# Encoder trunk on one core: where VectorE's low parts, convolution taps, gate blocks and edge zeros stand in the queues

## The chip, the cores and the metric

One core of a Trainium2 chip runs the whole trunk: two layers over 768 tokens, in float32 products that are put together from rounded high and low parts. The metric is device microseconds of one execution, as the median of several runs. Differences under about 0.2% (5 us) can't be told from no change.

## The reference, cut to what matters

```python
def trunk(x, ...):                       # x: (1, 256, 1024) and (1, 512, 1024), same weights
    for l in range(DEPTH):               # DEPTH = 2
        h = rms_norm(x, g_mix[l])
        q, k, v, u, gl = jnp.split(h @ w_in[l], splits, axis=-1)
        q = apply_axial_rope(rms_norm(q, g_q[l]), cos, sin)
        k = apply_axial_rope(rms_norm(k, g_k[l]), cos, sin)
        a = blocked_attention(q, k, v)   # 8 heads of 128, 2 kv heads, softmax over all keys
        c = conv_module(u, ...)          # a * sigmoid(g); depthwise conv of 31 taps;
                                         # layer norm over channels; silu; @ w_pw
        ga, gc = jnp.split(jax.nn.sigmoid(gl + b_gate[l]), 2, axis=-1)
        x = x + (ga * a + gc * c) @ w_out[l]
        gate, up = jnp.split(rms_norm(x, g_ffn[l]) @ w_gu[l], 2, axis=-1)
        x = x + (silu(gate) * up) @ w_down[l]
    return rms_norm(x, g_final)
```

## The kernel before

A product of two float32 matrices is made of three passes: high x high, low x high, high x low. ScalarE rounds a loaded weight tile of 128x1024 into its high part (line 211), and the low part, tile minus high, is written by VectorE (line 133) or GpSimd (line 214). `Unit.make` does this for one tile. `Weights` holds at most `N_WS` = 4 loaded tiles that are not yet split, and `split` counts a tile as used once its high and low parts have been issued.

Each layer has a mixing half and a feed-forward half. In the mixing half the program issues blocks in the order of the list `FILL`: `ag:j` makes the two halves of the input of convolution channel block j (128 channels), `gl:i` a gate block, and `k`, `v`, `q:i` the attention's inputs. The first seven blocks run alone. The other 22 are poured between the steps of the attention: one step for each head h and each token tile t (48 steps, named h0t0 to h7t5 in the tiles), with `FILL_US` microseconds of block work for each step. When `FILL` is used up, the output products of the convolution, `pw:0` to `pw:7`, are poured in its place.

An attention step issues its scores, then VectorE's row maximum, ScalarE's exponential, GpSimd's reciprocal of the sum (line 1332, tile `st`) and ScalarE's scaling. TensorE transposes the result (tile `T`, line 207) one step later.

The convolution of a channel block is 30 taps on VectorE, each one instruction over 783 columns (tile `L_y<-L_z`), after ScalarE did the first. Tile `L_z` holds the gated input with 15 zero columns at the start, between the two sequences and at the end. There are `N_Z` = 3 such tiles. When `ag_half` wants a fourth, it issues taps at once until the oldest convolution's last tap has been issued (the loop with `clock.tap()`), and then GpSimd writes the three strips of zeros of the new tile (line 803). Otherwise the taps come from `Clock.tick`: it counts TensorE's columns at 2400 to the microsecond as its time, adds up a cost for each VectorE instruction (elements / 960 plus 0.13 us; for a tap 783 / 960 + `TAP_MORE`), and issues taps as long as VectorE's sum is less than `TAP_AHEAD` = 1 us ahead.

After the eighth convolution `channel_norm` follows: mean (TensorE, tile `L_mean`), centring, squares, variance (TensorE, tile `L_var`), the spread of the reciprocal root, scaling, silu, and the split into `L_zsh` and `L_zsl`, which `pw:0` needs (tile `L_c`). When `pw:0` is reached and the norm is not done, `Clock.force` issues all that is left of it on the spot, ahead of any further TensorE work.

All engines run their own queue in the order in which the program issued. The quoted lines are those that the steps below touch most:

```python
while y.z_live >= N_Z:          # ag_half
    clock.tap()
...
for o in (0, PAD + NP, ZP - PAD):
    nc.gpsimd.memset(part["z"][:, o:o + PAD], 0.0)
...
self.clock.vector(n / 960.0 + (TAP_MORE if n == CONV_N else 0.13))     # Vector
```

Of the kernel before, what the change touches and what calls it, by code (L numbers as in the profile page):

```python
# [30 lines left out]
PAD = CK // 2  # L31
# [87 lines left out]
class Vector:  # L119
# [5 lines left out]
    def __getattr__(self, name):  # L125
        f = getattr(self.engine, name)

        def call(out, *args, **kw):
            n = 1
            for d in (args[0].shape if name == "tensor_reduce" else out.shape)[1:]:  # L130
                n *= d
            self.clock.vector(n / 960.0 + (TAP_MORE if n == CONV_N else 0.13))
            return f(out, *args, **kw)  # L133
# [22 lines left out]
def trunk(tc, x_in, x_tok, w_a, w_qkv, w_pw, w_out, w_gu, w_down, vecs, gqk, rope, y_out):  # L156
    nc = tc.nc
    clock = Clock()
    vector = Vector(nc.vector, clock)

    with ExitStack() as ctx:
# [15 lines left out]
        def U(name, dtype=F32):  # L177
            return UC(name, dtype)[:, :T]

        def Z(name, n=ZP, dtype=F32):  # L180
            return wpool.tile([P, n], dtype, name=name, tag="z", bufs=N_Z)
# [28 lines left out]
        def act(out, in_, func=AF.Copy, **kw):  # L210
            nc.scalar.activation(out, in_, func, **kw)  # L211

        def sub_lo(engine, lo, x, hi):
            engine.tensor_tensor(lo, x, hi.bitcast(F32), op=ALU.subtract)  # L214
# [6 lines left out]
        class Stage:  # L221


            def __init__(self, name, src):
                self.name, self.src, self.tile, self.last = name, src, None, None
# [5 lines left out]
        class Unit:  # L231
# [2 lines left out]

            def __init__(self, name, stages):
                self.name, self.stages, self.out, self.live = name, stages, None, False
                for stage in stages:
                    stage.last = self

            def make(self, engines):  # L240
                hi = wpool.tile([P, 1024], F32R, name="hi_" + self.name, tag="w", bufs=N_W)
                lo = wpool.tile([P, 1024], F32R, name="lo_" + self.name, tag="w", bufs=N_W)
                stage = self.stages[0].tile
                act(hi, stage)
                n = 1024 // len(engines)
                for i, e in enumerate(engines):
                    sl = slice(i * n, (i + 1) * n)
                    sub_lo(e, lo[:, sl], stage[:, sl], hi[:, sl])
                self.out = (hi, lo)

        class Quarter(Unit):

# [6 lines left out]
            def make(self, engines):  # L259
                src = self.quad.operand(self.m)  # L260
                both = wpool.tile([P, 1024], F32R, name="wq_" + self.name, tag="w", bufs=N_W)
                hi, lo = both[:, :512], both[:, 512:]
                act(hi, src)
                sub_lo(engines[0], lo, src, hi)
                self.out = (hi, lo)

        class Quad:

# [19 lines left out]
        class Weights:  # L288
# [36 lines left out]
            def split(self, engines=(nc.gpsimd,)):  # L325
                w = self.all[self.ready]
                while not self.here(w):
                    assert self.load()
                assert self.live + w.size + max(self.staged, N_WS) <= N_W
                self.live += w.size  # L330
                w.live = True
                w.make(engines)
                self.staged -= sum(stage.last is w for stage in w.stages)
                self.ready += 1
                self.next = max(self.next, clock.now + W_STEP[w.size - 1])

            def pump(self):
                while self.load():
                    pass
                if self.ready < len(self.all) and clock.now >= self.next:  # L340
                    w = self.all[self.ready]
                    if self.here(w) and self.live + w.size + max(self.staged, N_WS) <= N_W:
                        self.split(self.engines(w))
# [5 lines left out]
            def get(self, w):  # L349
                while w.out is None:  # L350
                    self.split(self.engines(self.all[self.ready]))
                return w.out

            def free(self, w):
# [60 lines left out]
        weights = Weights()  # L415
# [86 lines left out]
        def proj_two(ws, hT, s, names, parts=SPLITS):  # L502

            t0, n = parts[s]
            ps = [PS(name) for name in names]
            for k in range(KC):
                for w, o in zip(ws, ps):
                    for p, (a, b) in enumerate(PASSES):
                        mm(o[:, :n], w[a][:, k * P:(k + 1) * P], hT.cols(k, b, s),
                           k == 0 and p == 0, k == KC - 1 and p == 2)  # L510
                if k % 2 and k < KC - 1:
                    yield
            yield
            return ps
# [118 lines left out]
        def layer_blocks(l):  # L633
# [127 lines left out]
            def conv(j, z):  # L761
                wcol = lambda k: vcol(l, V_WDW, k * KC + j)

                def first():
                    y.y[j] = UC(nm(f"y{j}"))
                    act(y.y[j], z[:, :CONV_N], AF.Identity, scale=wcol(0), bias=vcol(l, V_BDW, j))
# [23 lines left out]
                def ready():  # L790
                    first()
                    clock.at(FIRST_AT[1], lambda: clock.waiting.append(taps))
                clock.at(FIRST_AT[0], ready)

            def ag_half(j, ws, w0, s, part):
                if s == 0:
                    while y.z_live >= N_Z:
                        clock.tap()
                    y.z_live += 1
                    part["sg"] = U(nm(f"sg{j}"))  # L800
                    part["z"] = Z(nm(f"z{j}"))
                    for o in (0, PAD + NP, ZP - PAD):
                        nc.gpsimd.memset(part["z"][:, o:o + PAD], 0.0)
                sg, z = part["sg"], part["z"]
                t0, n = SPLITS[s]
                y.norm.need(s)
                if l in TWO_AG and (j, s) == (0, 0):
                    pg, pa = yield from proj_two([ws[w0], ws[w0 + 1]], y.hT, s, [nm(f"ug{j}_{s}"), nm(f"ua{j}_{s}")])
                    act(sg[:, t0:t0 + n], pg[:, :n])
                else:  # L810
                    pg = yield from proj_a(ws[w0], y.hT, s, nm(f"ug{j}_{s}"))
                    act(sg[:, t0:t0 + n], pg[:, :n])
                    pa = yield from proj_a(ws[w0 + 1], y.hT, s, nm(f"ua{j}_{s}"))
                act(z[:, ZOFF[s]:ZOFF[s] + n], pa[:, :n])
                if s == 0:
                    return
                ws.free(w0, w0 + 1)

                def gate():
                    for s, (t0, n) in enumerate(SPLITS):  # L820
                        zz = z[:, ZOFF[s]:ZOFF[s] + n]
                        vector.tensor_tensor(zz, zz, sg[:, t0:t0 + n], op=ALU.mult)
                    conv(j, z)

                def sig(dt):
                    act(sg, sg, AF.Sigmoid)
                    clock.at(dt, gate)
                y.sig.append((True, sig))
# [11 lines left out]
            def gl_body(idx):  # L840
                def body(ws):
# [3 lines left out]
                    for s, (t0, n) in enumerate(SPLITS):  # L845
                        pg = yield from proj_a(ws[0], y.hT, s, nm(f"gl{idx}_{s}"))
                        act(sg[:, t0:t0 + n], pg[:, :n])
                        if s == 0 and FILL[-1] == f"gl:{idx}":
                            y.h_free = 1
# [9 lines left out]

            for b in FILL:  # L860
                kind, _, n = b.partition(":")
                n = int(n or 0)
# [434 lines left out]
        def attention(y):  # L1297
# [7 lines left out]
            def scores(n):  # L1305
# [22 lines left out]

                late = stream.done((l, FILL[-1]))
                jobs[n] = [  # L1330
# [55 lines left out]
            def fill():  # L1386
                goal[0] += FILL_US / 2
                if not stream.done((l, FILL[-1])):
                    stream.run(goal[0], (l, FILL[-1]))
                    if stream.done((l, FILL[-1])):  # L1390
                        goal[0] = stream.work
                        goal[0] += PW_START
                        y.late = clock.now + 8.0
                        y.h_free = 2
                        split_z(y)
                elif y.m_done:
                    goal[0] = max(goal[0] + (LATE_US - FILL_US) / 2, stream.work)
                    stream.run(goal[0], (l, f"pw:{min(y.m_done, PW_MAX) - 1}"))
# [21 lines left out]
        def channel_norm(y):  # L1420
# [59 lines left out]
            def scale(j):  # L1480
                def f():
                    for s, (t0, n) in enumerate(SPLITS):
                        sl = slice(YO[s], YO[s] + n)
                        vector.tensor_tensor(ys[j][:, sl], ys[j][:, sl], rstd[s][:, :n], op=ALU.mult)
                    if j in SILU_AT:
                        clock.at(0.5, lambda: silus(j))
# [126 lines left out]
        clock.drain()  # L1613


FILL = ["ag2", "k", "q:0", "gl:0", "ag:4", "ag:2", "ag:3", "gl:8", "v", "gl:9", "gl:1", "q:1", "ag:5", "ag:6",
        "gl:10", "gl:2", "q:2", "ag:7", "gl:3", "gl:14", "gl:12", "gl:4", "gl:11", "q:3", "gl:5", "gl:13", "gl:7",
        "gl:15", "gl:6"]
SILU_AT = (5, 7)
FIRST_AT = (1.2, 1.4)  # L1620
BURSTS = ((1, 7), (6, 4), (5, 2), (3,))
D_FIRST = (4.0, 6.0)
# [11 lines left out]
BEFORE = 7  # L1634
SIG_MAX = 3
SIG_LEFT = 25
FILL_US = 6.3
LATE_US = 3.7
PW_MAX = 10
PW_START = 3.0  # L1640
# [6 lines left out]
RSTD_AFTER = 5.4  # L1647
TABLES_AT = 16.0
TAP_AHEAD = 1.0
TAP_MORE = 0.13  # L1650
W_STEP = (0.9, 2.9)
A_EXP = 2.2
A_REC = (3.5, 2.5)
# [91 lines left out]
```

## Time and profile before

| | us |
|---|---|
| median of 3 runs | 2441.3 (2438.95 to 2444.44) |
| the profiled execution, its own time | 2443.3 |
| its span in the trace | 2441.5 |
| TensorE busy | 2226.4 (91%) |
| VectorE busy | 1876.5 (77%) |
| ScalarE busy | 1143.8 (47%) |
| GpSimd busy | 1068.2 (44%) |
| mean granted TensorE clock | 0.959 of full speed |

The span has four parts: layer 0's mixing half (to about 700 us), its feed-forward half (to about 1210), and the same two of layer 1. The waits of one layer's mixing half return in the other's almost to the tenth of a microsecond, so one layer is read and counted twice.

### The profile page before, as it was taken

To read this page: it belongs to the slowest core of one execution; us is meant where nothing else is said; L and a number is where in the kernel's file an instruction comes from. 1 tells how busy PE (TensorE), PEld (TensorE's weight loads), DVE (VectorE), ACT (ScalarE), POOL (GpSimd) and SP (SyncE) were. 2 spreads that over 40 slices of the span, in tenths; PEclk is the share of its full clock that TensorE was granted. 3 is DMA by queue.
4 is the path that set the end of the run, shared out by engine and by line. 5 is a ranking of instruction groups with operands and counts; after the bars stand their busy time and mean duration, and the time that the engine had idled before them with its cause. 6 is when DMAs were issued, how large, how long until landed. Compare 5 with 4: busy or idle time off the path is not lost. (4 is left out here: it accounts for less than half of the span.)

```text
span 2441.5 us, 34896 instructions
## 1 busy us (share of the span) xinstructions
PE 2226.4 (91%) x13276; PEld 2095.6 (86%) x13276; DVE 1876.5 (77%) x2484; ACT 1143.8 (47%) x2289; POOL 1068.2 (44%) x935
## 2 busy tenths in 40 slices
PE   8999869949979999999989998698699799999997
PEld 7989859848979999999988898596589799999997
DVE  5899768956387788798968897689553877987888
ACT  5446536555244444444443555465642444444443
POOL 3704132311256666666445142131112666666663
PEclk9999989969989999999999999899799899999998
DMA  4112111213312343343421111112142133333332
GB/s 165 61 57 69 66 39 63 77 43 113 133 49 90 121 144 116 124 145 113 152 85 61 63 63 57 50 63 72 54 146 101 35 121 127 124 130 137 122 123 87
DMA packets 72423, 229.59 MB, mean 94 GB/s; under 512 B 8128, under 2 KB 15296, under 8 KB 72256
## 3 DMA queue, kind: packets, MB, share of 16 engines
q1 hardware_dynamic: 72256, 227.37, 27.1%
q8 instruction: 104, 1.70, 0.3%
q14 instruction: 63, 0.52, 0.1%
HBM read 208.46 MB, written 18.87 MB: 93 GB/s over the span
## 5 line engine op out<-in xcount | busy, mean ns | idle before, releaser
L133 DVE SCALAR_TENSOR_TENSOR L_y<-L_z,vec,L_y 128x783 f32<-128x783 f32 x480 | 496.1, 1077 | 0.8
L214 POOL TENSOR_TENSOR wq_L_wgu_0m<-T_L_wgu,wq_L_wgu_0m 128x512 fp32r<-128x512 f32 x168 | 228.6, 1376 | 173.8 <-ACT wq_L_wgu_0m L211 173.8
L211 ACT ACTIVATE wq_L_wgu_0m<-T_L_wgu 128x512 fp32r<-128x512 f32 x168 | 102.7, 630 | 259.3 <-DVE T_L_wgu L133 208.7
L214 POOL TENSOR_TENSOR wq_L_wgu_0m<-st_L_wgu,wq_L_wgu_0m 128x512 fp32r<-128x512 f32 x126 | 179.3, 1425 | 43.4 <-ACT wq_L_wgu_0m L211 42.7
L203 PE MATMUL L_gl<-L_h1h,hi_L_wgl 128*128 128x512 f32 (+1 forms) x512 | 176.6, 345 | 0.0
L203 PE MATMUL L_gl<-L_h1h,lo_L_wgl 128*128 128x512 f32 (+1 forms) x512 | 173.2, 338 | 0.0
L203 PE MATMUL L_gl<-L_h1l,hi_L_wgl 128*128 128x512 f32 (+1 forms) x512 | 172.9, 338 | 0.0
L203 PEld LDWEIGHTS L_gl<-L_h1h,lo_L_wgl 128*128 128x128 f32 x512 | 97.0, 189 | 11.0
L203 PEld LDWEIGHTS L_gl<-L_h1l,hi_L_wgl 128*128 128x128 f32 x512 | 97.2, 190 | 9.2
L203 PEld LDWEIGHTS L_gl<-L_h1h,hi_L_wgl 128*128 128x128 f32 x512 | 97.0, 190 | 9.1
L203 PE MATMUL L_c<-L_zsl,hi_L_wpw 128*128 128x256 f32 (+1 forms) x256 | 89.2, 348 | 9.5 <-DVE L_zsl L133 9.5
L203 PE MATMUL L_c<-L_zsh,hi_L_wpw 128*128 128x256 f32 (+1 forms) x256 | 92.1, 360 | 4.6 <-ACT L_zsh L211 4.6
L203 PE MATMUL L_ug<-L_h1h,lo_L_wu 128*128 128x256 f32 (+1 forms) x256 | 89.0, 348 | 2.8 <-DVE lo_L_wu L133 2.8
L133 DVE TENSOR_TENSOR L_dl<-L_silu,L_dh 128x384 fp32r<-128x384 f32 x80 | 59.5, 783 | 41.0 <-ACT L_dh L211 41.0
L203 PE MATMUL L_ug<-L_h1h,hi_L_wu 128*128 128x256 f32 (+1 forms) x256 | 90.6, 354 | 0.0
L203 PE MATMUL L_ua<-L_h1h,lo_L_wu 128*128 128x256 f32 (+1 forms) x256 | 88.6, 346 | 1.4 <-DVE lo_L_wu L133 1.4
L203 PE MATMUL L_ua<-L_h1h,hi_L_wu 128*128 128x256 f32 (+1 forms) x256 | 89.7, 350 | 0.0
L203 PE MATMUL L_ug<-L_h1l,hi_L_wu 128*128 128x256 f32 (+1 forms) x256 | 89.5, 349 | 0.0
L211 ACT ACTIVATE wq_L_wgu_0m<-st_L_wgu 128x512 fp32r<-128x512 f32 x126 | 78.5, 623 | 22.8 <-POOL wq_L_wgu_0m L214 19.8
L203 PE MATMUL L_c<-L_zsh,lo_L_wpw 128*128 128x256 f32 (+1 forms) x256 | 88.9, 347 | 0.0
L203 PE MATMUL L_ua<-L_h1l,hi_L_wu 128*128 128x256 f32 (+1 forms) x256 | 88.1, 344 | 0.0
L203 PE MATMUL L_o<-L_mTlo,hi_L_wo 128*128 128x384 f32 x256 | 86.4, 338 | 0.0
(1630 smaller groups left out, 7626.7 us busy)
## 6 DMA issues: line engine op xcount, KB each, us to landing
st_L_wgu<-w_gu SPq DMA_DIRECT2D x88, 512.0 KB, 3.5
st_L_wu<-w_a SPq DMA_DIRECT2D x32, 512.0 KB, 3.5
st_L_wgl<-w_a SPq DMA_DIRECT2D x32, 512.0 KB, 3.5
st_L_wqkv<-w_qkv SPq DMA_DIRECT2D x24, 512.0 KB, 3.5
st_L_wpw<-w_pw SPq DMA_DIRECT2D x16, 512.0 KB, 3.5
st_L_wo<-w_out SPq DMA_DIRECT2D x16, 512.0 KB, 3.6
g_dram<-L_sgl SPq DMA_DIRECT2D x16, 384.0 KB, 3.0
L_gj<-g_dram SPq DMA_DIRECT2D x16, 384.0 KB, 3.8
```

What stands on the lines that cost most here:

```text
L133: return f(out, *args, **kw)
L203: nc.tensor.matmul(out, lhsT, rhs, start=start, stop=stop)
L211: nc.scalar.activation(out, in_, func, **kw)
L214: engine.tensor_tensor(lo, x, hi.bitcast(F32), op=ALU.subtract)
```

## The change

VectorE's low parts of weight tiles are no longer issued together with the high part, but 1.6 us of the program's clock later, or when the tile is first asked for; a loaded tile counts as used only then. In `FILL`, `ag:6` comes one block later and `ag:7` two blocks later. The zeros at the edges of `L_z` are written by VectorE. A tap costs 0.11 us less in the program's count, so taps are issued at a closer pace. `FILL_US` goes from 6.3 to 6.5.

```diff
 class Unit:
     def __init__(self, name, stages):
         self.name, self.stages, self.out, self.live = name, stages, None, False
+        self.low = lambda: None
     def make(self, engines):
         act(hi, stage)
         n = 1024 // len(engines)
-        for i, e in enumerate(engines):
-            sl = slice(i * n, (i + 1) * n)
-            sub_lo(e, lo[:, sl], stage[:, sl], hi[:, sl])
+        def low():
+            for i, e in enumerate(engines):
+                sl = slice(i * n, (i + 1) * n)
+                sub_lo(e, lo[:, sl], stage[:, sl], hi[:, sl])
+            weights.used(self)
         self.out = (hi, lo)
+        if engines == (vector,):
+            self.low = clock.later(LO_AFTER, low)
+        else:
+            low()
 class Weights:
     def split(self, engines=(nc.gpsimd,)):
         w.make(engines)
-        self.staged -= sum(stage.last is w for stage in w.stages)
+    def used(self, w):
+        self.staged -= sum(stage.last is w for stage in w.stages)
     def get(self, w):
         while w.out is None:
             self.split(self.engines(self.all[self.ready]))
+        w.low()
         return w.out
 def ag_half(j, ws, w0, s, part):
         for o in (0, PAD + NP, ZP - PAD):
-            nc.gpsimd.memset(part["z"][:, o:o + PAD], 0.0)
+            vector.memset(part["z"][:, o:o + PAD], 0.0)
-FILL = [..., "q:1", "ag:5", "ag:6", "gl:10", "gl:2", "q:2", "ag:7", "gl:3", "gl:14", "gl:12", ...]
+FILL = [..., "q:1", "ag:5", "gl:10", "ag:6", "gl:2", "q:2", "gl:3", "gl:14", "ag:7", "gl:12", ...]
+LO_AFTER = 1.6
-FILL_US = 6.3
+FILL_US = 6.5
-TAP_MORE = 0.13
+TAP_MORE = 0.02
```

## Rows read from the trace of the kernel before

**Rows 1.** Stretches, layer 0: length, busy PE, PEld, DVE, ACT, POOL; PEclk, DMA, GB/s
```profile
45.00:158.00 113.00, 111.12 (x721) 100.76 (x721) 99.05 (x110) 48.18 (x118) 45.88 (x49) 1.00 0.19 63
158.00:320.00 162.00, 155.06 (x1078) 143.52 (x1077) 136.54 (x181) 93.64 (x213) 54.35 (x59) 0.98 0.18 59
320.00:346.00 26.00, 4.66 (x28) 3.81 (x27) 19.66 (x22) 3.60 (x11) 5.60 (x9) 0.68 0.08 25
346.00:484.00 138.00, 138.00 (x860) 123.48 (x859) 113.30 (x142) 81.76 (x170) 35.48 (x36) 0.99 0.21 73
484.00:521.00 37.00, 7.09 (x28) 5.19 (x27) 25.54 (x47) 18.80 (x27) 3.54 (x5) 0.58 0.05 15
```
**Rows 2.** TensorE's waits, whole span: who for whom, us in total, times, longest
```profile
PE L_h3t0T L207 <- ACT L_h3t0p L211: 42.6, 2, 21.3
PE L_var L203 <- DVE L_sq L133: 40.3, 2, 20.1
PE L_h1t5T L207 <- ACT L_h1t5p L211: 13.0, 2, 6.5
```
**Rows 3.** Timeline 320 to 350 us (start, length, instruction, idle before and who ended it)
```profile
324.03 15.20 DVE L133 SCALAR_TENSOR_TENSOR L_y<-L_z,vec,L_y 128x783 f32<-128x783 f32 x16
339.29 0.20 POOL L803 MEMSET L_z<- 128x15 f32 x3 [19.29 <-DVE L_y L133]
344.59 0.54 POOL L1332 TENSOR_TENSOR L_h3t0st<-L_h3t0st,nones 128x1 f32<-128x1 f32 x1
345.72 0.69 PE L207 MATMUL L_h3t0T<-ident,L_h3t0p 128*128 128x128 f32 x2 [21.34 <-ACT L_h3t0p L211]
...
348.39 0.42 DVE L133 TENSOR_REDUCE L_h3t1st<-L_h3t1s 128x1 f32<-128x256 f32 x1
```
**Rows 4.** Timeline 247 to 260 us, VectorE and GpSimd, ahead of h1t5T's wait
```profile
247.66 8.59 DVE L133 SCALAR_TENSOR_TENSOR L_y<-L_z,vec,L_y 128x783 f32<-128x783 f32 x9
256.31 0.20 POOL L803 MEMSET L_z<- 128x15 f32 x3 [12.74 <-DVE L_y L133]
258.12 0.68 DVE L133 TENSOR_REDUCE L_h1t5st<-L_h1t5s 128x1 f32<-128x512 f32 x1
```
**Rows 5.** VectorE's waits from 20 to 486 us, the low parts of weight tiles
```profile
DVE lo_L_wgl L133 <- ACT hi_L_wgl L211: 22.3, 9, 6.2
...
DVE lo_L_wu L133 <- ACT hi_L_wu L211: 6.4, 5, 2.4
DVE lo_L_wqkv L133 <- ACT hi_L_wqkv L211: 5.8, 5, 2.1
```
**Rows 6.** Timeline 483 to 516 us: last convolution's end, and pw:0's first product
```profile
483.41 0.96 DVE L133 TENSOR_TENSOR L_ysum<-L_ysum,L_y 128x783 f32<-128x783 f32 x1
...
515.24 0.58 PE L203 MATMUL L_c<-L_zsh,hi_L_wpw 128*128 128x256 f32 x1 [2.30 <-ACT L_zsh L211]
```
**Rows 7.** Timeline of VectorE: taps with GpSimd silent, and beside its rope products
```profile
113.27 10.46 DVE L133 SCALAR_TENSOR_TENSOR L_y<-L_z,vec,L_y 128x783 f32<-128x783 f32 x11
...
218.97 3.66 DVE L133 SCALAR_TENSOR_TENSOR L_y<-L_z,vec,L_y 128x783 f32<-128x783 f32 x3
```
**Rows 8.** Timeline of TensorE: two products of 512 columns, one after the other
```profile
412.16 0.39 PE L203 MATMUL L_h4t3s<-L_kThi,L_q2Tlo 128*128 128x512 f32 x1
412.39 0.39 PE L203 MATMUL L_h4t3s<-L_kTlo,L_q2Thi 128*128 128x512 f32 x1
```
**Rows 9.** Timeline: a scaled softmax tile and its transposition, and one without slack
```profile
409.47 0.72 ACT L211 ACTIVATE L_h4t2p<-L_h4t2p,L_h4t2st 128x512 f32<-128x512 f32 x1 [0.74 <-POOL L_h4t2st L1332]
417.59 0.60 PE L207 MATMUL L_h4t2T<-ident,L_h4t2p 128*128 128x128 f32 x4
...
164.54 0.44 PE L207 MATMUL L_h0t0T<-ident,L_h0t0p 128*128 128x128 f32 x2 [0.45 <-ACT L_h0t0p L211]
```
**Rows 10.** Short instructions: the zeros now (min/median/max in ns), VectorE's small copy
```profile
L803 POOL MEMSET L_z<- x48: 110/112/113, 18.6 to 1550.2; 128x15 f32 x48
508.86 0.17 DVE L133 COPY L_vs<-L_var 128x6 f32<-128x6 f32 x1 [2.81 <-PE L_var L203]
```

More of the change, by code (lines that the diff above doesn't have):

```diff
@@ L265, in make @@
                 self.out = (hi, lo)
+                weights.used(self)
         class Quad:
@@ L1613, in trunk @@
         clock.drain()
-FILL = ["ag2", "k", "q:0", "gl:0", "ag:4", "ag:2", "ag:3", "gl:8", "v", "gl:9", "gl:1", "q:1", "ag:5", "ag:6",
-        "gl:10", "gl:2", "q:2", "ag:7", "gl:3", "gl:14", "gl:12", "gl:4", "gl:11", "q:3", "gl:5", "gl:13", "gl:7",
+FILL = ["ag2", "k", "q:0", "gl:0", "ag:4", "ag:2", "ag:3", "gl:8", "v", "gl:9", "gl:1", "q:1", "ag:5",
+        "gl:10", "ag:6", "gl:2", "q:2", "gl:3", "gl:14", "ag:7", "gl:12", "gl:4", "gl:11", "q:3", "gl:5", "gl:13", "gl:7",
         "gl:15", "gl:6"]
 SILU_AT = (5, 7)
+LO_AFTER = 1.6
 FIRST_AT = (1.2, 1.4)
```

## The prediction

> **What bounds the kernel now.** I read the share of busy time first. TensorE is busy for most of the span, so the question is where it is not. The busy time by stretch shows two holes in layer 0's mixing half: from 320 to 346 us TensorE works 4.66 of 26 us, from 484 to 521 it works 7.09 of 37 [rows 1]. TensorE's waits name them: 21.3 us for the transposition of step h3t0 and 20.1 us for the variance, and a third of 6.5 us at h1t5; each comes twice with the same length, once a layer [rows 2].
>
> Then the timeline of the first hole. GpSimd sat idle for 19.29 us in front of the zeros, until VectorE ended 16 taps in one run of 15.20 us; behind the zeros stood the reciprocal for h3t0, which ended at 345.13, and TensorE went on at 345.72 [rows 3]. The program explains the run: `ag:7` wanted a fourth tile, so taps were issued without pause until the oldest was free, and the zeros wait for the last of them. At h1t5 the shape is another one: GpSimd was through with its zeros at 256.51, but VectorE reached the row maximum only at 258.12, behind nine taps [rows 4]. There the run of taps is the cause, and moving the zeros alone would leave it.
>
> The second hole is the end of a VectorE chain: the last convolution is summed at 484.37, the norm follows, and `pw:0` starts at 515.24 [rows 6]. TensorE had nothing to do in it, since `force` puts the norm ahead of all else. So the mixing half ends when VectorE's convolutions end. Is VectorE saturated before? From 45 to 484 us it is busy 99.05 + 136.54 + 19.66 + 113.30 = 368.6 of 439 us [rows 1]: 70.4 us idle. Of these, 34.5 are waits of low parts for their high part, in 19 places [rows 5].
>
> **The change part by part, for one layer.**
>
> *Zeros on VectorE.* They need no wait there: the last tap of the old tile stands ahead of them in the same queue. GpSimd's last work before the zeros ended at 339.29 - 19.29 = 320.0, and from the zeros' end to the reciprocal's end it took 345.13 - 339.49 = 5.6 us [rows 3]. Without the zeros the reciprocal ends near 326, and TensorE, which came at 345.72 - 21.34 = 324.4, goes on near 326.5: it saves 19. New on VectorE are 24 short writes. The trace has none of them there; the nearest rows are 0.112 us on GpSimd and 0.17 us for a small copy on VectorE [rows 10]. I take 0.1, as they would run back to back, so 2.4 us of VectorE a layer (bounds 0, where VectorE is idle, to 4.1). [...]
>
> *Later gate blocks, closer taps.* These decide whether the runs of taps remain. A tap counts 783/960 + 0.13 = 0.946 us in the program, after the change 0.836. The program's microsecond is short: 512 columns are 0.213 of it, while products follow each other at 0.23 [rows 8], a factor of 1.08. So a tap is issued per 1.02 us now, per 0.90 after. A tap lasts 0.95 with GpSimd silent and 1.22 beside rope products [rows 7]. The planner has thus left VectorE air, and will leave it next to none. The run at h3t0 ends with the last tap of the fifth convolution, so at least 150 - 16 = 134 taps had gone ahead of it; 13% more are 17, as many as the run. And `ag:7` stands two blocks of 7.68 program us later. So I expect no runs at `ag:6` and `ag:7`, and the 6.5 us of h1t5 go too. TensorE reaches `pw:0` 19 + 6.5 = 25.5 us earlier, near 484 - 25.5 = 458.5. `FILL_US` 6.5 brings the 222.7 program us of blocks into 34.3 steps in place of 35.3: one step less ahead of `pw:0`, some 1.5 us.
>
> *Low parts later.* In the 1.6 us VectorE takes taps that wait for nothing. Of 34.5 us of waits I expect 5 to stay where ScalarE itself is late: 30 us of VectorE. A loaded tile is given back 1.6 us later; with four of them held and one used per 7.7 us of block work this is hidden. Without that cover it costs up to 1.6 us per block, but TensorE shows no wait for weights of that kind among its long waits.
>
> *Where the stall goes.* Now VectorE is late next. The convolutions' end moves from 484.4 by -30 (low parts), -6.3 (its own idle in the first hole, 26 - 19.66 [rows 1]), +2.4 (zeros), -2 (one step's VectorE work less), to 448.5. That leaves about 34 us idle in front of it, which closer taps can fill in part; between nothing and half (17) I take 9: 440. The norm took 515.2 - 484.4 = 30.8 us when forced [rows 6]; partly mixed with the attention I give it 36: `pw:0` at about 476 in place of 515.2, and TensorE, there at 457, waits some 19 where it waited 30. Gain 39 a layer, less 1 us for new small waits behind a fuller VectorE queue: 38, for two layers 76. All else (both feed-forward halves) stays.
>
> The rope rows bound the closer taps: 1.22 against 0.95 [rows 7]. [...]
>
> The sum is made against the profiled span of 2441.5 us (its own time 2443.3; the median of the runs is 2441.3, which I start from): 2441.3 - 76 = **2365**.
>
> **The rivals.**
>
> *Half of it.* The runs of taps remain, or VectorE's idle time stays in new places. TensorE then goes on at 326.5, but meets h3t1's maximum behind the 16 taps. Now that maximum starts 9 us after the run's end, of which some 3 are left without the hole, so it would be near 342, its tile ready near 345; TensorE, one step further (6.3 program us of blocks and the step's own products, 8 us or so), comes near 335 and waits 10. Saved 9 of the 21; if a quarter of the 30 us of low parts comes out too, 7, it is 16 a layer: 2409. For it: ScalarE's own write of `L_z` also needs the tile free. Against: 13% more taps.
>
> *The wait moves whole.* VectorE is the bound, its idle can't be had, and the variance waits longer by what the transposition no longer does: about 2440. Against it: 70 us idle.
>
> *The norm is hidden.* Convolutions end near 425, the norm runs among attention steps, and only about 5 us remain at `pw:0` at 462: 53 a layer and the clock's return (0.68 and 0.58 granted in the holes [rows 1]), 2331. For it: the program's count, 240 x 0.11 x 1.08 = 28.5 us less for the taps. Against it: 365 us of VectorE work in 380.
>
> *Slower.* The row maxima stand behind taps that VectorE hasn't worked off. A step's slack between scaling and transposition goes from 7.4 us (410.19 to 417.59) down to none [rows 9]. Some 35 steps a layer run beside taps, 70 in all; each wait of X costs 70 X, and from 76/70 = 1.1 us on the kernel is slower. At two taps too many, 1.9 us, it is 133 - 76 = 57 more: 2498. Against it: TensorE's waiting lets VectorE catch up.
>
> **How the numbers follow.** Forecast 0.55 (2345 to 2390), half of it 0.20 (2395 to 2420), hidden norm 0.15 (2320 to 2345), whole move 0.04, slower 0.06. Range 2325 to 2415: it leaves out the last two, a part of the half and of the hidden norm. About 0.2% can be told from no change: faster 0.90, same 0.04, slower 0.06.
>
> **What would show it.** GpSimd has no wait for `L_y` in front of zeros; h3t0T waits under 3 us and h1t5T under 1. VectorE's waits for high parts of weights fall from 34.5 to about 5. Runs of more than eight taps before `ag:6` and `ag:7` are gone. The last sum of a convolution is near 440, the first `L_c` near 476, and TensorE's wait there near 19. Wrong would be: transpositions waiting for ScalarE in most steps (slower), or the variance's wait grown by 20 us (whole move).

## The result and the profile after

The changed kernel takes 2350.5 us (median, 2347.6 to 2353.1) beside 2442.6 for the kernel before: a ratio of 0.9625, 95% interval 0.9606 to 0.9643, 92 us less. The forecast was 2365 with a range of 2325 to 2415. The profiled execution spans 2351.4 us where that of before spanned 2441.5, and the mean granted TensorE clock is 0.978 where it was 0.959.

The stretches of layer 0 in the kernel after, with the cuts moved to its own events (start:end, length, busy PE, PEld, DVE, ACT, POOL with the number of instructions, granted clock, DMA share, GB/s):

```profile
...
320.00:346.00 26.00, 25.31 (x160) 22.70 (x160) 26.00 (x35) 12.23 (x27) 10.53 (x8) 1.00 0.23 72
...
436.00:476.00 40.00, 33.74 (x195) 28.89 (x193) 27.77 (x46) 28.90 (x47) 4.03 (x6) 0.95 0.26 91
```

The first hole is gone: from 320 to 346 TensorE works 25.31 of 26 us where it worked 4.66 [rows 1], at a granted clock of 1.00 where it was 0.68. The second one has shrunk: TensorE idles 6.3 of the 40 us from 436 to 476, between the convolutions' end and `pw:0`, where it had idled 29.9 of the 37 us from 484 to 521 [rows 1].

TensorE's waits from 45 us to the first `L_c`, kernel after (who for whom: us in total, times, longest); the answer to [rows 2]:

```profile
PE L_rstd L207 <- DVE L_rb L133: 4.0, 1, 4.0
PE L_h4t4T L207 <- ACT L_h4t4p L211: 3.8, 1, 3.8
PE L_h1t2T L207 <- ACT L_h1t2p L211: 2.4, 1, 2.4
...
PE L_q0T L207 <- DVE L_kTlo L133: 2.2, 1, 2.2
PE L_h0t0T L207 <- ACT L_h0t0p L211: 1.9, 1, 1.9
PE L_ua L203 <- DVE lo_L_wu L133: 1.1, 1, 1.1
```

The three waits of [rows 2], 21.3, 20.1 and 6.5 us a layer, are not in the list. In their place are small ones in new places. What became of the end of the mixing half stands in the timeline of the kernel after (start, length, engine, instruction, idle before and who ended it), the answer to [rows 6]:

```profile
434.80 0.97 DVE L133 TENSOR_TENSOR L_ysum<-L_ysum,L_y 128x783 f32<-128x783 f32 x1
...
467.40 0.60 PE L207 MATMUL L_h5t3T<-ident,L_h5t3p 128*128 128x128 f32 x4
...
471.96 1.54 PE L207 MATMUL L_rstd<-ident,L_rb 128*128 128x128 f32 x6 [3.96 <-DVE L_rb L133]
...
475.81 0.58 PE L203 MATMUL L_c<-L_zsh,hi_L_wpw 128*128 128x256 f32 x1 [2.30 <-ACT L_zsh L211]
...
481.12 0.58 PE L203 MATMUL L_c<-L_zsl,hi_L_wpw 128*128 128x256 f32 x1 [4.73 <-DVE L_zsl L133]
```

The last convolution is summed at 435.8 (before 484.4), `pw:0` starts at 475.8 (before 515.2), and TensorE still transposes attention steps at 467.4; its last gate block ends at 467.6. Around the norm it waits 3.96 + 2.30 + 4.73 = 11.0 us, the last of the three behind the first `L_c`.

Where the time of a layer came from is read from four windows: from 45 us to the first `L_c`, and from there to the first product of the feed-forward half. First the kernel before:

```profile
45.00:515.20 470.20, 414.91 (x2703) 376.03 (x2702) 388.29 (x485) 240.31 (x528) 143.38 (x156) 0.94 0.18 60
515.20:690.30 175.10, 163.09 (x948) 151.40 (x949) 85.56 (x133) 79.17 (x140) 43.34 (x37) 0.96 0.31 105
```

and the kernel after:

```profile
45.00:475.80 430.80, 411.94 (x2698) 374.31 (x2696) 387.81 (x501) 243.60 (x529) 146.84 (x137) 0.99 0.21 67
475.80:645.80 170.00, 162.92 (x955) 150.97 (x956) 85.24 (x135) 81.38 (x145) 44.49 (x38) 0.97 0.31 103
```

Up to `L_c` TensorE idles 18.9 us in place of 55.3, which is 36.4 of the 39.4 us gained; the other 3.0 are the same products done faster (2698 beside 2703 of them, granted clock 0.99 for 0.94). Behind `L_c` another 5.1 us, nearly all of it idle time: 7.1 in place of 12.0. That makes 44.5 a layer. The first feed-forward product of layer 1 starts at 1808.7 in place of 1899.2, which is 90.5 sooner; both layers gain alike, and the feed-forward halves give nothing.

### The profile page after: what moved, and what is told of

Same layout as the page of the kernel before. It is cut to its first block, busy times and chain, and to the rows that moved or that the text cites. A ratio compares the mean times of both kernels' runs of the same rounds, so it can differ in the third digit from the quotient of the medians.

```text
span 2351.4 us, 34909 instructions
## 1 busy us (share of the span) xinstructions
PE 2221.8 (94%) x13276; PEld 2092.6 (89%) x13276; DVE 1875.1 (80%) x2532; ACT 1154.5 (49%) x2299; POOL 1073.9 (46%) x887
## 5 line engine op out<-in xcount | busy, mean ns | idle before, releaser
L133 DVE SCALAR_TENSOR_TENSOR L_y<-L_z,vec,L_y 128x783 f32<-128x783 f32 x480 | 498.8, 1078 | 1.6
L203 PE MATMUL L_ug<-L_h1h,hi_L_wu 128*128 128x256 f32 (+1 forms) x256 | 90.5, 353 | 0.0
L203 PE MATMUL L_o<-L_mThi,hi_L_wo 128*128 128x384 f32 x256 | 86.9, 339 | 0.0
```

What stands on the lines that cost most here:

```text
L203: nc.tensor.matmul(out, lhsT, rhs, start=start, stop=stop)
```

## The experiments

The theory after the result: the mixing half ends when VectorE's chain of convolutions and norm ends, so what counts is how densely VectorE is fed with taps and how little of its queue waits. Closer taps and later low parts are then the change, and the zeros and the order of `FILL` only move stalls. The rival takes each part at the size that the prediction wrote beside it: zeros 19 us of TensorE's time a layer, low parts 30 us of VectorE, closer taps 9. Each part but `FILL_US` was made alone on the kernel before (names with s_), then each was undone alone in the kernel after (u_). Medians stand against 2443.4 to 2443.8 for the kernel before.

**Zeros alone.**

```diff
-                        nc.gpsimd.memset(part["z"][:, o:o + PAD], 0.0)
+                        vector.memset(part["z"][:, o:o + PAD], 0.0)
```

> The kernel before with the zeros alone moved to VectorE. First theory (VectorE's convolutions set when pw:0 can start, and the runs of taps are still there): GpSimd no longer waits, h3t0T goes on some 19 us sooner, but h3t1's maximum stands behind the 16 taps and h1t5T keeps its 6.5 us; the convolutions' end moves by VectorE's own idle time in the hole at most, 6 us a layer, so about 2430 us, with the variance's wait longer than 20.1. Rival (each hole of TensorE is worth its length): 19 us a layer, about 2403.

Measured: 2438.4 us, ratio 0.9975 (0.9966 to 0.9985): 5 us in two layers, where the rival has 38; the theory expected about 2430. The convolutions end at 483.65 (before 484.4). Timeline of this kernel in the old hole:

```profile
325.15 18.03 DVE L133 SCALAR_TENSOR_TENSOR L_y<-L_z,vec,L_y 128x783 f32<-128x783 f32 x19
...
330.00 0.69 PE L207 MATMUL L_h3t0T<-ident,L_h3t0p 128*128 128x128 f32 x2 [3.27 <-ACT L_h3t0p L211]
...
343.25 0.12 DVE L133 MEMSET L_z<- 128x15 f32 x3
343.27 0.39 ACT L211 ACTIVATE L_z<-L_ua 128x256 f32<-128x256 f32 x1 [11.62 <-DVE L_y L133]
343.30 0.42 DVE L133 TENSOR_TENSOR L_h2t2m<-L_h2t2av,L_sgl 128x256 f32<-128x256 f32 x1
...
343.78 0.80 PE L203 MATMUL L_h3t2s<-L_kThi,L_q1Thi 128*128 128x512 f32 x1 [7.94 <-DVE L_h2t2m L133]
```

and its waits of TensorE in layer 0:

```profile
PE L_var L203 <- DVE L_sq L133: 18.7, 1, 18.7
PE L_h3t2s L203 <- DVE L_h2t2m L133: 7.9, 1, 7.9
PE L_h1t5T L207 <- ACT L_h1t5p L211: 7.1, 1, 7.1
PE L_mean L203 <- DVE L_ysum L133: 4.9, 1, 4.9
PE L_h3t0T L207 <- ACT L_h3t0p L211: 3.3, 1, 3.3
```

The wait for h3t0 fell from 21.3 to 3.3, much as the prediction worked out, and h1t5 keeps its wait (7.1), as it also said. But the run of taps is still there (19 in 18.03 us), and the next thing in VectorE's queue behind it, `L_h2t2m`, now stops TensorE for 7.9 us at h3t2; ScalarE's write of `L_z` waits 11.6 us for the last tap. What TensorE gains at h3t0 is gone by the norm, since the convolutions end only 0.7 us sooner: besides the 7.9, a wait of 4.9 for the sum is new, and up to the first `L_c` TensorE's products take 420.4 us in place of 414.9, some of them at the lower granted clock of the old hole, 0.81 from 320 to 346 us in the window below. `L_c` starts 0.8 us sooner. And behind the run VectorE starves, in the kernel before (340 to 360 us):

```profile
340.00:360.00 20.00, 14.28 (x68) 12.08 (x69) 4.97 (x9) 8.33 (x20) 5.96 (x8) 0.75 0.20 66
```

and in this one:

```profile
320.00:346.00 26.00, 14.79 (x73) 12.18 (x72) 25.27 (x32) 5.58 (x14) 8.09 (x7) 0.81 0.04 13
346.00:360.00 14.00, 14.00 (x75) 12.48 (x74) 6.34 (x11) 9.17 (x20) 1.08 (x2) 0.86 0.33 121
```

VectorE is busy 4.97 of 20 and 6.34 of 14 us there. By the program, a forced run of 16 taps puts VectorE's sum 16 x 0.946 = 15 us ahead of the planner's time, and no tap is issued until that time has caught up. So a run costs twice: TensorE stands behind it, and afterwards VectorE has nothing to do. That the planner's sum is the reason is read from the code and not measured; the idle time is.

**Low parts alone.** `Unit.make` as in the change, with `LO_AFTER` = 1.6, and nothing else:

```diff
+                if engines == (vector,):
+                    self.low = clock.later(LO_AFTER, low)
+                else:
+                    low()
```

> The kernel before with the low parts alone issued 1.6 us later. First theory (a tap goes out at the pace of the program's count, so air on VectorE alone is not turned into earlier taps): VectorE's waits for high parts fall from 34.5 us to about 5, but the last convolution ends at most 10 us sooner, about 2425. Rival (the prediction's term as it stands): the convolutions' end moves by the whole 30 us, about 2381.

Measured: 2427.8 us, ratio 0.9934 (0.9919 to 0.9948), 16 us. VectorE's waits for high parts fall from 36.4 to 11.7 us (both with the `wpw` tiles), but the convolutions end only 5 us sooner, at 479.1, and the first hole stays, as TensorE's wait shows:

```profile
PE L_h3t0T L207 <- ACT L_h3t0p L211: 19.8, 1, 19.8
```

From 45 us to the convolutions' end VectorE still idles 63.0 us, where it had idled 70.5: most of the waits that were taken out came back as other idle time, as the theory had it of a queue that the planner fills too slowly.

**Closer taps alone.**

```diff
-TAP_MORE = 0.13
+TAP_MORE = 0.02
```

> The kernel before with only the cost of a tap lowered to 0.836 in the program's count. First theory (the pace sets the convolutions' end): the run of 16 taps ahead of h3t0 shrinks below 8 and h3t0T's wait with it, the last convolution ends some 20 us sooner, about 2401. Rival (VectorE's waits for high parts hold it back as before): VectorE falls behind, small waits at the transpositions take the place of the runs, within 10 us of 2441.

Measured: 2381.2 us, ratio 0.9733 (0.9714 to 0.9753): 63 us, two thirds of the whole change from one constant, and more than the 40 or so of the theory. The last sum of a convolution in the timeline, then GpSimd's zeros at the first tile that it waits for and at `ag:7`, then the end of TensorE's block work and `pw:0`:

```profile
433.91 0.97 DVE L133 TENSOR_TENSOR L_ysum<-L_ysum,L_y 128x783 f32<-128x783 f32 x1
```

```profile
130.33 0.20 POOL L803 MEMSET L_z<- 128x15 f32 x3 [21.92 <-DVE L_y L133]
...
326.69 0.20 POOL L803 MEMSET L_z<- 128x15 f32 x3
```

```profile
479.11 0.60 PE L207 MATMUL L_h5t4T<-ident,L_h5t4p 128*128 128x128 f32 x4
...
485.28 0.58 PE L203 MATMUL L_c<-L_zsh,hi_L_wpw 128*128 128x256 f32 x1 [4.91 <-ACT L_zsh L211]
```

The convolutions end at 434.9, as early as in the kernel after, and no run of more than five taps is left after 200 us. GpSimd's waits for tiles come to 48.6 us, but 41.6 of them lie at 130 and 150 us, ahead of the attention steps, where the kernel before has 24.4 and 17.8 and no long wait of TensorE follows. At `ag:7` the zeros, still on GpSimd, find their tile free, and h3t0 costs TensorE 4.1 us in place of 21.3: without the run in front of them they need not move.

And yet `pw:0` starts 9.5 us later than in the kernel after, though the convolutions end no later. Here TensorE's last gate block ends at 479.3 and the first `L_c` follows 6.0 us behind it. The traces of all kernels fall in two groups by this, in layer 0. In the five with the old pace (before, and the runs s_zeros, s_low, s_order and u_taps) the first `L_c` follows the convolutions' end by 29.4 to 30.9 us. In the nine with a closer pace it follows that by anything from 40.0 to 64.8, but TensorE's last gate block by 6.0 to 9.7. So the theory's bound, VectorE's chain, holds with the old pace; with a closer one it is mostly TensorE's own work that sets `pw:0`, with a short rest of the norm behind it.

**Order of the gate blocks alone.**

```diff
-FILL = [..., "ag:5", "ag:6", "gl:10", "gl:2", "q:2", "ag:7", "gl:3", "gl:14", "gl:12", ...]
+FILL = [..., "ag:5", "gl:10", "ag:6", "gl:2", "q:2", "gl:3", "gl:14", "ag:7", "gl:12", ...]
```

> The kernel before with only ag:6 and ag:7 standing later in the order of blocks. First theory: fewer taps are outstanding when the fourth tile is asked for, the runs are half as long, and both holes before pw:0 shrink by half, but the last convolution ends no sooner, so the variance waits longer: about 2435. Rival (holes count by their length): 14 us a layer, about 2413.

Measured: 2397.5 us, ratio 0.981 (0.9796 to 0.9825), 46 us, more than either theory expected (2435 and 2413). GpSimd's zeros at `ag:7`, then the old hole as a window:

```profile
340.02 0.20 POOL L803 MEMSET L_z<- 128x15 f32 x3 [7.74 <-DVE L_y L133]
```

```profile
320.00:346.00 26.00, 26.00 (x157) 23.35 (x157) 24.25 (x31) 12.20 (x26) 2.92 (x6) 0.96 0.19 66
```

GpSimd still waits for this tile, 7.74 us in place of 19.29, and yet TensorE has no hole: with two more blocks in between there is no run of taps in front. The convolutions end at 460.4, 24 us sooner than before at the same pace: from 45 us up to their end VectorE idles 45.3 us in place of 70.5, and its waits for high parts fall from 36.4 to 20.2 us though no low part was moved. So the order does not only move stalls, as the theory had it: the runs had kept VectorE idle too. TensorE arrives at the norm sooner as well and still waits 18.7 us for the variance.

**The zeros back on GpSimd, in the kernel after.**

```diff
-                        vector.memset(part["z"][:, o:o + PAD], 0.0)
+                        nc.gpsimd.memset(part["z"][:, o:o + PAD], 0.0)
```

> The changed kernel with the zeros back on GpSimd. First theory (the runs of taps were the cause of the holes, the zeros only stood behind them): no runs are left from step h1t0 on, so GpSimd's waits for L_y stay short there; at most 5 us lost, 2351 to 2356. Rival (the zeros' own wait is worth 19 us a layer, as the prediction had it): about 2389.

Measured: 2351.4 us, ratio 0.9622 (0.9608 to 0.9637), no difference from the kernel after. GpSimd's zeros at the first tile that it waits for, and at `ag:7`:

```profile
130.51 0.20 POOL L816 MEMSET L_z<- 128x15 f32 x3 [20.59 <-DVE L_y L133]
...
338.33 0.20 POOL L816 MEMSET L_z<- 128x15 f32 x3
```

Its waits come back only at 130 and 147 us, ahead of the attention steps, and cost nothing there; where the old hole was, the zeros find their tile free.

**Low parts issued with the high part again, in the kernel after.**

```diff
-                if engines == (vector,):
-                    self.low = clock.later(LO_AFTER, low)
-                else:
-                    low()
+                low()
```

> The changed kernel with the low parts issued together with the high parts again. First theory (with the closer taps VectorE has little air, so waits for high parts now push the convolutions' end): the waits come back to 25 us or more a layer and the end moves by half of them or more, 2375 to 2400. Rival (the pace of the count sets the end, as before the change, where this edit alone gave 16 us): about 2365.

Measured: 2386.9 us, ratio 0.977 (0.9754 to 0.9786). Undoing it costs 36 us, where doing it alone brought 16. VectorE's waits for high parts from 20 to 446 us, then the last sum in the timeline:

```profile
DVE lo_L_wgl L133 <- ACT hi_L_wgl L211: 15.6, 6, 5.5
...
DVE lo_L_wu L133 <- ACT hi_L_wu L211: 6.0, 3, 2.9
DVE lo_L_wqkv L133 <- ACT hi_L_wqkv L211: 5.4, 5, 2.0
```

```profile
444.59 0.97 DVE L133 TENSOR_TENSOR L_ysum<-L_ysum,L_y 128x783 f32<-128x783 f32 x1
```

These waits come to 27.0 us, against 8.4 in the kernel after. The convolutions end at 445.6 in place of 435.8, the first `L_c` starts at 488.4 in place of 475.8, the feed-forward half at 660.9 in place of 645.8: 9.8, 12.6 and 15.1 us later. TensorE's last gate block ends 12.5 us later, too (480.1 for 467.6): up to `L_c` it idles 26.4 us in place of 18.9, and its products take 417 us in place of 412. So the low parts' worth is not one of the convolutions' end alone.

**The old pace of the taps, in the kernel after.**

```diff
-TAP_MORE = 0.02
+TAP_MORE = 0.13
```

> The changed kernel with the cost of a tap back at 0.946 in the count. First theory (pace sets the convolutions' end): no runs at ag:6 and ag:7, but the last convolution ends 20 us or more later than 435.8, near 455, and the norm is forced again with 18 us of wait at the variance; about 2390. Rival (the later blocks and the low parts do it without the pace): under 2365.

Measured: 2392.5 us, ratio 0.9792 (0.9777 to 0.9806): undoing it costs 42 us. The convolutions end at 461.1, 25 us later than in the kernel after, and TensorE waits 18.7 us for the variance again. A run of eight taps (7.64 us) is left ahead of `ag:7`, which the expectation had ruled out; no wait of TensorE stands behind it.

**The old order, in the kernel after** (the `FILL` diff above, reversed).

> The changed kernel with ag:6 and ag:7 at their old places. First theory (either of the two edits ends the runs; closer taps alone already had none): within 6 us of 2350.5. Rival (both are needed once TensorE no longer stalls): runs of 8 taps or more return before ag:6 or ag:7, the wait at h1t5T or h3t0T with them, 2365 to 2380.

Measured: 2351.6 us, ratio 0.9624 (0.9609 to 0.9638), nothing. With the closer pace the tiles come free in time in either order. Pace and order each take the hole at h3t0 away but for 4.1 and 2.0 us (63 and 46 us alone), so either can stand in for the other there; no kernel with the old pace ends its convolutions before 460.

**FILL_US back to 6.3, in the kernel after.**

```diff
-FILL_US = 6.5
+FILL_US = 6.3
```

> The changed kernel with FILL_US back at 6.3. First theory (one attention step more stands ahead of pw:0, and nothing else changes): the waits at the spread of the norm and at pw:0 shrink by at most the step's 1.5 us a layer; 2346 to 2354, not to be told apart from 2350.5. Rival (the pour's pace decides whether the norm is done when the blocks run out): 5 us a layer or more to either side, below 2341 or above 2360.

Measured: 2355.7 us, ratio 0.9639 (0.9624 to 0.9653), whose interval overlaps that of the kernel after; the median is 5 us above. It lies between the first theory's range and the rival's, so it is inconclusive.

**Low parts and closer taps, nothing else**, on the kernel before: the two diffs above together, with zeros on GpSimd, the old order and `FILL_US` 6.3.

> The kernel before with two edits only: low parts later, and a tap counted at 0.836. Zeros on GpSimd, ag:6 and ag:7 and FILL_US as before. First theory (these two carry the change; undone one at a time they cost 36 and 42 us, the others nothing): 2345 to 2357, as fast as the changed kernel. Rival (the edits that cost nothing when undone alone stand in for each other, and one of them is needed): a run of 8 taps or more and a wait at h3t0T return, 2362 or more.

Measured: 2342.2 us (2339.5 to 2344.4), ratio 0.9584 (0.9568 to 0.96). That is 101 us, more than 16 + 63 = 79, and 8 us better than the whole change, with intervals of the ratio that don't overlap; the theory that named these two parts had expected 2345 to 2357 and was 3 us too cautious. From 45 to 436 us, first this kernel, then the kernel after:

```profile
45.00:436.00 391.00, 379.49 (x2510) 346.40 (x2510) 366.07 (x447) 214.43 (x484) 142.93 (x150) 0.99 0.19 63
```

```profile
45.00:436.00 391.00, 378.39 (x2507) 345.61 (x2506) 360.24 (x456) 214.90 (x483) 142.81 (x131) 0.99 0.20 65
```

VectorE is fuller by 6 us with the same TensorE work done. The convolutions end at 428.9, `L_c` starts at 472.7, the feed-forward half at 639.9. Set against closer taps alone (434.9, 485.3, 658.9), the low parts bring 6.0 us by the convolutions' end, 12.6 by `L_c` and 19.0 by the feed-forward half: they keep working after the last tap, where the norm and the row maxima share VectorE's queue with them. From 430 to 660 us VectorE waits 15.9 us for high parts with closer taps alone and 2.5 here. Why zeros, order and `FILL_US` together cost 8 us, though each undone alone brings nothing that can be told, stays open.

**Less to do for VectorE**, in the kernel after: taps 28 and 29 of each channel block are left out, 16 of 240 a layer.

```diff
-                taps = [tap(k) for k in range(1, CK - 1)] + [last]
+                taps = [tap(k) for k in range(1, CK - 3)] + [last]
```

> The changed kernel with the convolution's taps 28 and 29 left out in every channel block, so its output is another one: 16 taps, some 15 us of VectorE, less a layer. First theory (VectorE's convolutions still set when pw:0 starts, but only by the 11 us that TensorE still waits there): the last convolution ends some 15 us sooner than 435.8, and 6 to 11 us a layer are gained, 2328 to 2340. Rival (VectorE is the bound in full): 15 us a layer, about 2320. Second rival (TensorE's own work is the bound): within 5 us of 2350.5.

Measured: 2335.8 us, ratio 0.9559 (0.9545 to 0.9573), 7.3 us a layer for 16 x 0.95 = 15.2 us of VectorE. The last sum, then the window from 45 us to the first `L_c`:

```profile
403.55 1.18 DVE L133 TENSOR_TENSOR L_ysum<-L_ysum,L_y 128x783 f32<-128x783 f32 x1
```

```profile
45.00:469.50 424.50, 409.61 (x2688) 372.15 (x2686) 375.40 (x491) 243.96 (x527) 143.69 (x136) 0.98 0.19 64
```

The convolutions end 31 us sooner, twice the work that was left out and twice what was expected, yet the first `L_c` moves only from 475.8 to 469.5. TensorE idles 14.9 us up to there (18.9 in the kernel after): of the time by which VectorE is done sooner, most finds TensorE at work on blocks that have to be done anyway. `L_c` again follows TensorE's last gate block by 6.0 us. VectorE is no longer the bound in full.

**A still closer pace**, in the kernel after.

```diff
-TAP_MORE = 0.02
+TAP_MORE = -0.05
```

> The changed kernel with a tap counted at 0.766 in the place of 0.836, 0.83 us of TensorE's time, less than a tap lasts. First theory (VectorE is busy for 92% of the stretch up to the last convolution, so a closer pace only makes its queue longer): the last convolution ends at most 8 us sooner and the waits of transpositions for ScalarE grow by about as much, 2344 to 2358. Rival (pace still sets the end): another 10 us a layer, about 2330. Second rival (the slower case of the prediction, row maxima stuck behind taps): over 2365.

Measured: 2363.9 us, ratio 0.9677 (0.9661 to 0.9693), 13 us slower than the kernel after. This missed both: the first theory's range (2344 to 2358), and the rival's bound of 2365 by a microsecond, though in the rival's direction. The last sum, then TensorE's longest waits from 45 to 484 us, then the window to the first `L_c`:

```profile
421.84 0.96 DVE L133 TENSOR_TENSOR L_ysum<-L_ysum,L_y 128x783 f32<-128x783 f32 x1
```

```profile
PE L_c L203 <- ACT L_zsh L211: 5.6, 1, 5.6
PE L_h1t2T L207 <- ACT L_h1t2p L211: 2.7, 1, 2.7
PE L_h2t4T L207 <- ACT L_h2t4p L211: 2.2, 1, 2.2
...
```

```profile
45.00:483.60 438.60, 415.28 (x2694) 376.50 (x2692) 392.71 (x509) 243.62 (x529) 141.96 (x136) 0.98 0.19 62
```

The convolutions end 13 us sooner than in the kernel after, and `pw:0` starts 8 us later. TensorE idles 23.3 us up to there in place of 18.9, spread over some fifteen waits of which none is over 5.6 us: the prediction's rival "slower" in a mild form. Its products also take 3.3 us more, at a granted clock of 0.98 where it was 0.99. Up to the feed-forward half the two layers account for 8.4 us, and the profiled spans differ by 9.3; where the rest of the 13 goes isn't settled.

## Why the prediction was right, and where its steps were not

**Direction and size: right. The bound: not as said.** The kernel is 92 us faster where 76 were forecast, the time came from the two places named, and the convolutions' end (435.8, forecast 440) and the first `L_c` (475.8, forecast 476) stand where the forecast had them. But it had TensorE at `pw:0` at 457, with 19 us to wait there for VectorE's chain. TensorE's last gate block ended at 467.6, and `L_c` followed 8.2 us later. So VectorE's chain was the bound before the change and is hardly the bound after it, and that `L_c` came out to 0.2 us is luck.

**Zeros: the step that failed.** The prediction took the wait that ended last, GpSimd's 19.29 us in [rows 3], for the cause of the hole and wrote "it saves 19" beside the moved zeros. In its sum these 19 only bring TensorE to `pw:0` sooner; the gain goes by the convolutions' end, where the hole stands with -6.3 and the zeros with +2.4. Alone the moved zeros took 18.0 us out of the wait at h3t0, but they moved the convolutions' end by 0.7 us and not by 3.9, and brought 2.7 a layer; in the kernel after they bring nothing. The run of taps was the cause; whatever stands behind it, zeros or `L_h2t2m`, is only who shows it. The prediction had this reading at h1t5 ("there the run of taps is the cause") and not at h3t0. The rival "half of it" priced the zeros without the end of the runs at some 9 us a layer, still too much, because it did not follow the gain to the norm.

**Closer taps: the mis-sized term.** "Between nothing and half (17) I take 9" was less than a third of what the low parts got. Alone the closer pace ends the convolutions 49.5 us sooner and is worth 63 us, beside 92 for the whole; undone, it costs 42. That the runs at `ag:6` and `ag:7` would end was right: the longest run after 200 us is of five taps, and h1t5 has left the list of TensorE's waits.

**Low parts: right on the waits, wrong on what they are worth.** VectorE's waits in the kernel after, 20 to 440 us, the answer to [rows 5]:

```profile
DVE lo_L_wgl L133 <- ACT hi_L_wgl L211: 6.5, 3, 4.7
...
DVE lo_L_wu L133 <- ACT hi_L_wu L211: 1.2, 1, 1.2
...
DVE lo_L_wqkv L133 <- ACT hi_L_wqkv L211: 0.7, 1, 0.7
```

8.4 us stay, where 5 were expected of 34.5. But 30 us of VectorE off the convolutions' end was wrong: alone the later low parts moved it by 5, undone in the kernel after by 9.8. The sum came near 440 by luck, because two terms were off in opposite directions: too much for the low parts, too little for the pace.

**The norm and TensorE's arrival: two more misses that cancel.** The convolutions ended 4 us earlier than said and the norm took 475.8 - 435.8 = 40.0 us in place of 36. TensorE was forecast at `pw:0` at 457 with a wait of 19; it still worked at 467.4 and waited 11.0. The 1 us allowed for new small waits is the term that was too small: the waits at h4t4, h1t2, `q0T`, h0t0 and `L_ua` come to 11.4 us, and the last three of them were 2.4 us before.

**"All else stays" was 5 us a layer short.** Behind `L_c` the idle time fell from 12.0 to 7.1 us; the wait for h6t0's transposition, 5.7 us in layer 0 before, is gone. These 5.1 us are most of the difference between 44.5 and the forecast's 38; the rest is the 1 us taken off for small waits, since up to `L_c` 39.4 us came where 39 stood. Of the 39.4, 3.0 are products at a higher granted clock, which the forecast left to the rival "hidden norm".

**The rivals.** "The wait moves whole" did not come, but the zeros alone came close to it. "The norm is hidden", at a chance of 0.15, has the mechanism that came: most of the norm ran among attention steps, and 8.2 us remained behind TensorE's last gate block, beside the rival's 5 and the forecast's 19. The time stayed above its 2331 (an estimate) because TensorE came to `pw:0` at 467.6 and not at 457; the low parts and the pace without the rest, with 6.0 us left there, give 2342. "Slower" is seen at the next closer pace. `FILL_US`, put at 1.5 us a layer, is not to be told from nothing.

## What to carry to other kernels

The instruction that ends a long wait last may only stand behind the cause: before a part is given the price of the wait, look at what it is queued behind, and ask who comes next in that queue when it is gone. A long chain in the background of one engine wants an even pace: of the parts made alone here the pace was worth most (63 us). Of the three counts tried for a tap the middle one was best (0.836 program us; 0.946 cost 42 us, 0.766 cost 13): at the slow pace the chain ended 25 us later and the norm had to be waited for, at the fast one TensorE's short waits grew (it idles 23.3 us up to `L_c` in place of 18.9). Once the chain ends early enough, the bound is elsewhere, and a still earlier end buys little: 31 us sooner with the taps left out moved the first `L_c` by 6.3. Savings on a queue are worth what they find there: 25 us a layer of waits taken from a queue with air in it were worth 16 us in two layers, and 19 us a layer taken from a full one were worth 36.

## What the runs showed of the hardware

The zeros, 128x15 each, as the kernel after has them on VectorE (ns shortest/median/longest, first and last start):

```profile
L133 DVE MEMSET L_z<- x48: 71/71/71, 20.9 to 1500.9; 128x15 f32 x48
```

They take 71 ns each, against 112 ns on GpSimd [rows 10] and 100 in the forecast: 1.7 us a layer.

The 480 taps of the whole run lasted 1077 ns each in the mean before and 1078 after, by the page's groups of instructions. The prediction set the taps beside rope products (1.22 us against 0.95, [rows 7]) as a bound on the closer pace. By the mean of all taps nothing of it came; the taps that run beside GpSimd's work were not timed apart.
